# Output projections that take the activations as the stationary operand, with a token-major residual

## The chip, the cores and the metric

The kernel runs on one core of one Trainium2 chip, as one program. The metric is the device time of one execution in microseconds (us). Half speed of TensorE's clock is 1.2 GHz, full speed 2.4 GHz; the profile shows the granted clock as a share of the full one.

## The reference

Two transformer blocks are applied to one sequence of 256 tokens with 2048 features, all in fp32. The first block's shift, scale and gate vectors come from a condition vector `c`. Cut to what matters here:

```
mod = silu(c) @ ada_w + ada_b                 # 6 vectors of 2048: sh_a, sc_a, g_a, sh_f, sc_f, g_f
h = rms_norm(x, pre) * (1 + sc_a) + sh_a
y = mixer(h)                                  # w_in, latent and differential heads, then concat @ w_o
x = x + g_a * rms_norm(y, attn_post)
h = rms_norm(x, ffn_pre) * (1 + sc_f) + sh_f
u = conv3(h @ w_up); y = (gelu(u_gate) * u_val) @ w_down
x = x + g_f * rms_norm(y, ffn_post)
h = rms_norm(x, norm_g)                       # second block
x = x + concat(heads_a, heads_b)(h @ w_in_2) @ w_out
return rms_norm(x, final_g)
```

The matrices that matter are `w_o` (2048x2048), `w_down` (5632x2048) and `w_out` (2048x2048): the output projections. rms_norm needs the sum of squares over the 2048 features of each token.

## The kernel before

All weights come as one stream, `wstream`, in 704 pieces of 512 KB, each eight blocks of 128x128, in the order of use, through SP's DMA queue (`fetch`, L268) into twelve buffers `raw`. `convert` splits each chunk of four blocks into a rounded part `hi` (ACT, L290) and a remainder `lo` (DVE, L291), four chunks ahead of the matmuls; six such pairs of buffers exist. The activations have the same two parts, side by side in one tile of 128 features by 512 (256 tokens rounded, 256 tokens remainder). A product takes three passes: hi by hi, hi by remainder, lo by hi.

Three helpers issue matmuls. `mm3` (L329 to L331) holds the weight block still and streams 256 tokens three times. `mmw` (L337, L338) does the same with one 512-wide and one 256-wide pass. `job_n` (L421 to L423) holds 128 tokens of the activations still and streams 512 columns of weights; only the value projection uses it. `job_t` goes column by column of the output, `job_ko` keeps several columns open and goes over the contraction tiles `kt` outside, so that work can start when only the first `kt` exist.

The residual `x` is kept feature-major, as the products of `mm3` come out: eight tiles of 128 features by two times 256 tokens. An output projection comes in two halves over its contraction: `y_first` copies the first half from PSUM to `accy` (L1131), `y_second` adds the second half (`y_stats`, L1154). `y_stats` then makes three sets of squares and products (ACT L1158 and L1163, DVE L1159), which TensorE sums over features by matmuls with a matrix of ones (L1168), and scales `y` by gate and norm weight (L1171). For each pair of output columns this is one group, and the sums of all groups gather in one PSUM tile `st`. `post` turns them by small selection matmuls (L1180) into per-token numbers, takes two inverse roots (`rsqrt_fast`, L552 to L557) and broadcasts them (L567). `make_h` with `x_new` (L1224 to L1226) then updates `x` and makes the input `h` of the next projection, two feature tiles at a time, at every even `kt` of the `job_ko` that starts w_up and w_in_2 (ACT L1211, L1212 and DVE L1213 in the first, L1206 and L1207 in the second). The last stage, w_out, adds into `x` (L1413, L1426), squares (L1427), sums by ones (L580), scales (L1434), and `fin` multiplies eight tiles and stores them (L1448, L1449).

The gate vectors are made among other work: `ada_late` is woven into w_o, `ada_dve` with `ada_fold` (L526) into w_up.

Work of the engines is recorded in program order: each engine does its instructions strictly in the order in which a generator of the body issued them (`tick` advances such generators as matmuls are issued).

Of the kernel before, what the change touches and what calls it, by code (L numbers as in the profile page):

```python
# [13 lines left out]
F32 = mybir.dt.float32  # L14
# [3 lines left out]
AF = mybir.ActivationFunctionType  # L18
# [3 lines left out]
P = 128  # L22
T = 256
# [8 lines left out]
KO = 4  # L32
LATE, VSLOT = 4, (1,2, 3)
# [101 lines left out]
class Body:  # L135
# [293 lines left out]

    def ada_pe(self, slots, n, done=None, vec=()):  # L430
# [5 lines left out]
        def unit(m, kt):  # L436
            def fn(wt, o):
# [8 lines left out]
                if last and kt == KT - 1 and e == n * 128:  # L446
                    self.spawn(self.ada_end(box["ps"], slots, n, done), "ada")
# [62 lines left out]
    def ada_dve(self, part, t0):  # L510
        out, box = [], {}
        for kt in range(KT):
            def fn(wt, o, kt=kt):
# [3 lines left out]
                if kt == KT - 1 and o * 128 + wt.shape[-1] == 512:  # L517
                    self.spawn(self.ada_fold(box["acc"], part * 16 + t0), "ada")
# [3 lines left out]
    def ada_fold(self, acc, col):  # L522
# [536 lines left out]
    def p_attn(self):  # L1059
# [59 lines left out]
    def y_job(self, mat, kts, x, ko, ev):  # L1119
        cols = [128 * i for i in range(16)]  # L1120
        out = self.job_ko(mat, cols[:ko], kts, x, ev) if ko else []
        return out + self.job_t(mat, cols[ko:], kts, x, lambda i, ps: ev(ko + i, ps))

    def y_first(self, mat, kts, x, ko=0):
        self.accy = None

        def ev(i, ps):
            if i == 0:
                self.accy = [None] * 8
            self.accy[i // 2] = d = self.g()  # L1130
            self.nc.scalar.copy(d, ps)  # L1131
        return self.y_job(mat, kts, x, ko, ev)

    def y_second(self, mat, kts, x, part, wname, ko=0):
        nc = self.nc
        V, S = nc.vector, nc.scalar

        def start():
            self.gw = self.s(16)
            V.tensor_tensor(out=self.gw, in0=self.mod[:, part * 16:part * 16 + 16], in1=self.vec(wname), op=ALU.mult)  # L1140
            self.st = self.ps()
            self.load_sqrt()

        def ev(i, ps):
            self.spawn(self.y_stats(i, ps), "y")
        return self.call(start) + self.y_job(mat, kts, x, ko, ev)

    def y_stats(self, i, ps):
        nc = self.nc
        V, S = nc.vector, nc.scalar  # L1150
        y = self.accy[i // 2]
        hv = [slice(h * T, h * T + T) for h in range(2)]
        for a in (hv if i == 14 else [slice(0, 512)]):
            V.tensor_add(y[:, a], y[:, a], ps[:, a])  # L1154
        yq, zq, xz = self.w(), self.w(), self.w()
        for h, a in enumerate(hv):
            gw = self.gw[:, i + h:i + h + 1]
            S.activation(zq[:, a], y[:, a], AF.Square, scale=gw)  # L1158
            V.scalar_tensor_tensor(out=xz[:, a], in0=y[:, a], scalar=gw, in1=self.x[i // 2][:, a],  # L1159
                                   op0=ALU.mult, op1=ALU.mult)  # L1160
            if i == 14 or h == 1:
                b = a if i == 14 else slice(0, 512)
                S.activation(yq[:, b], y[:, b], AF.Square)  # L1163
        if i != 14:
            yield
        for h, b in enumerate(hv):
            for j, a in enumerate((yq, zq, xz)):
                nc.tensor.matmul(self.st[32 * j:32 * j + 32, :T], self.cst("ones", 0, 32), a[:, b],  # L1168
                                 start=i + h == 0, stop=i + h == 15, tile_position=(0, 32 * j))
        for h, a in enumerate(hv):  # L1170
            S.activation(y[:, a], y[:, a], AF.Identity, scale=self.gw[:, i + h:i + h + 1], bias=0.0)  # L1171

    def post(self):
        nc = self.nc
        V = nc.vector
        part = self.w()
        V.tensor_copy(part[:96, :T], self.st[:96, :T])
        ps = self.ps()
        for t in range(2):
            nc.tensor.matmul(ps[:, t:t + 6:2], part[:96, t * 128:t * 128 + 128], self.cst("sel", 1, 4)[:96],  # L1180
                             start=True, stop=True)
        ry = self.rsqrt_fast(ps[:, 0:2], 2, 1.0 / D)
        t = self.s(2)
        V.tensor_tensor(out=t, in0=ps[:, 2:4], in1=ry, op=ALU.mult)
# [585 lines left out]
```

## Time and profile before

| | |
|---|---|
| median of 3 runs | 1730.6 us (1730.32 to 1730.95) |
| the profiled execution, its span | 1729.1 us, 1727.3 us |
| busy: PE, DVE, ACT | 98%, 70%, 55% of the span |
| mean granted clock of TensorE | 0.988 |
| HBM read, written | 373.06 MB, 2.10 MB |

The span runs from the first to the last recorded event; what lies around it is 1.8 us. PE's busy time counts matmuls as pipelined work; the duration of one matmul in a row is its latency, so rates are read from the distance of the starts. The rows used are in the section ahead of the prediction.

### The profile page before, as it was taken

Reading aid. Unit: us, or ns where it says so; the run is one execution under the profiler, and the core shown is the slowest. Engines: PE = TensorE matmul, PEld = TensorE weight load, DVE = VectorE, ACT = ScalarE, POOL = GpSimd, SP = SyncE. Lnnn points to the kernel's source line nnn. Section 1 sums busy time; section 2 is a strip of 40 time slices with the busy share of each in tenths; the row PEclk is TensorE's granted clock in tenths of the full one; section 3 lists DMA queues with packets and bytes.
Section 4 is the critical chain, followed back from the end, with each engine's and each line's share of the span. In section 5 each row is a group of like instructions: output and inputs, shape, how many; then the busy total and the mean of one; then the engine's idle time right before and its main releaser. Section 6 shows DMA issues by size and latency. Waiting matters only on the chain.

```text
span 1727.3 us, 31993 instructions
## 1 busy us (share of the span) xinstructions
PE 1687.2 (98%) x12008; PEld 1468.4 (85%) x12008; DVE 1215.4 (70%) x2472; ACT 948.5 (55%) x1975; POOL 8.9 (1%) x25
## 2 busy tenths in 40 slices
PE   6999999999989999999999999999989999999997
PEld 4778877788779888899998888899989888888996
DVE  7666678777578978865568777755576767777654
ACT  4444458654567766654456666654544445555553
POOL 0000000000000000000000000000000000000000
PEclk8999999999989999999999999999989999999998
DMA  9978885879945766666676765555445773443431
GB/s 381 338 283 302 305 292 184 286 304 375 345 161 185 235 223 219 221 224 217 204 232 223 226 196 185 194 172 173 168 145 184 255 252 110 142 138 136 141 128 50
DMA packets 104987, 377.24 MB, mean 218 GB/s; under 512 B 11776, under 2 KB 12032, under 8 KB 104832
## 3 DMA queue, kind: packets, MB, share of 16 engines
q1 hardware_dynamic: 103968, 373.51, 62.6%
q8 instruction: 94, 1.54, 0.4%
q10 hardware_dynamic: 864, 1.69, 0.3%
q14 instruction: 61, 0.50, 0.1%
HBM read 373.06 MB, written 2.10 MB: 217 GB/s over the span
## 4 chain that ended last, share of the span: by engine, by line
PE 96%; DVE 2%; DMA 1%; ACT 0%; issue 0%; ACTq 0%; DVEq 0%
PE ps L337 24%; PE ps L329 14%; PE ps L330 14%; PE ps L331 14%; PE ps L338 12%; PE ps L444 4%; PE ps L421 2%; PE ps L422 1%; PE ps L423 1%; PE ps L646 1%; PE ps L1168 1%; PE ps L1639 1%; PE ps L952 1%; PE ps L1660 1%; PE ps L1589 1%; PE ps L769 1%
## 5 line engine op out<-in xcount | busy, mean ns | idle before, releaser
L290 ACT CAST hi<-raw 128x512 fp32r<-128x512 f32 x989 | 608.9, 620 | 585.8 <-PE ps L330 270.4
L291 DVE TENSOR_TENSOR lo<-raw,hi 128x512 fp32r<-128x512 f32 x989 | 673.8, 689 | 315.6 <-ACT hi L290 308.8
L337 PE MATMUL ps<-g,hi 128*128 128x512 f32 x1744 | 619.0, 399 | 0.0
L329 PE MATMUL ps<-g,hi 128*128 128x256 f32 x1968 | 569.2, 290 | 4.0 <-ACT g L1211 2.1
L330 PE MATMUL ps<-g,hi 128*128 128x256 f32 x1968 | 559.3, 284 | 0.0
L331 PE MATMUL ps<-g,lo 128*128 128x256 f32 x1968 | 558.0, 284 | 0.0
L338 PE MATMUL ps<-g,lo 128*128 128x256 f32 x1744 | 489.5, 281 | 0.0
L329 PEld LDWEIGHTS ps<-g,hi 128*128 128x128 f32 x1968 | 378.3, 193 | 44.6 <-issue 18.0
L337 PEld LDWEIGHTS ps<-g,hi 128*128 128x128 f32 x1744 | 327.4, 188 | 80.4 <-issue 1.7
L330 PEld LDWEIGHTS ps<-g,hi 128*128 128x128 f32 x1968 | 379.2, 193 | 5.7 <-issue 4.3
L331 PEld LDWEIGHTS ps<-g,lo 128*128 128x128 f32 x1968 | 378.8, 193 | 2.9 <-issue 2.1
L338 PEld LDWEIGHTS ps<-g,lo 128*128 128x128 f32 x1744 | 329.6, 189 | 0.0
L487 DVE SCALAR_TENSOR_TENSOR w<-raw,csil,w 128x512 f32<-128x512 f32 x105 | 78.6, 749 | 30.9 <-DMA raw<-wstream 30.2
L444 PE MATMUL ps<-raw,cz 128*32 128x512 f32 (+1 forms) x608 | 79.9, 564 | 0.0
L884 DVE TENSOR_TENSOR g<-g,ps 128x512 f32<-128x512 f32 (+1 forms) x48 | 31.8, 664 | 43.7 <-PE ps L331 43.6
L421 PE MATMUL ps<-hi,g 128*128 128x512 f32 (+1 forms) x136 | 51.8, 381 | 1.1 <-ACT g L845 1.1
L422 PE MATMUL ps<-lo,g 128*128 128x512 f32 (+1 forms) x136 | 49.9, 367 | 0.0
L423 PE MATMUL ps<-hi,g 128*128 128x512 f32 (+1 forms) x136 | 49.8, 366 | 0.0
L1239 ACT ACTIVATE w<-w,vt 128x256 f32<-128x256 f32 x80 | 47.7, 599 | 1.9 <-DVE w L345 1.6
L345 DVE TENSOR_TENSOR w<-w,ps 128x256 f32<-128x256 f32 x109 | 45.0, 415 | 0.8 <-ACT w L344 0.8
L649 ACT ACTIVATE w<-ps,t 128x256 f32<-128x256 f32 (+1 forms) x80 | 33.5, 429 | 19.9 <-DVE t L1031 15.6
L344 ACT COPY w<-ps 128x256 f32<-128x256 f32 x109 | 40.1, 369 | 0.0
(266 smaller groups left out, 1257.4 us busy)
## 6 DMA issues: line engine op xcount, KB each, us to landing
raw<-wstream SPq DMA_DIRECT2D x704, 512.0 KB, 4.3
g<-xt SPq DMA_DIRECT2D x8, 256.0 KB, 5.5
out<-g SPq DMA_DIRECT2D x8, 256.0 KB, 2.4
g<-ropes ACTq DMA_DIRECT2D x2, 256.0 KB, 2.5
vt<-vecs ACTq DMA_DIRECT2D x1, 459.5 KB, 4.2
ct<-cst ACTq DMA_DIRECT2D x1, 265.0 KB, 3.1
g<-w ACTq DMA_DIRECT2D x1, 256.0 KB, 3.2
g<-pos SPq DMA_DIRECT2D x1, 160.0 KB, 3.8
```

What stands on the lines that cost most here:

```text
L290: self.nc.scalar.copy(hi[:, :n], src)
L291: self.nc.vector.tensor_sub(lo[:, :n], src, hi[:, :n].bitcast(F32))
L329: i = mm(o, hi, x[:, :T], start=first, stop=False)
L330: mm(o, hi, x[:, T:], start=False, stop=False)
L331: mm(o, lo, x[:, :T], start=False, stop=last)
L337: mm(ps, hi, x, start=first, stop=False)
L338: mm(ps[:, T:], lo, x[:, :T], start=False, stop=last)
L421: mm(ps[t][:, c], xh, hi, start=f and o == 0, stop=False)
L422: mm(ps[t][:, c], xh, lo, start=False, stop=False)
L423: mm(ps[t][:, c], xl, hi, start=False, stop=l and c.stop == w)
L444: mm(box["ps"][32 * q:32 * q + 32, o * 128:e], self.cz[:, a:a + 32], wt, start=first, stop=last and kt >= 12 and e == n * 128, tile_positi ...
L487: V.scalar_tensor_tensor(out=a, in0=w, scalar=c, in1=a, op0=ALU.mult, op1=ALU.add)
```

## The change

The three output projections go to a new helper `job_y`, of the form of `job_n`: 128 tokens of activations are stationary and 512 columns of weights move, six matmuls for four blocks, 1216 blocks in all. Outputs come out token-major, so the residual is kept token-major (`xn`, eight tiles of 128 tokens by 512 features), and is loaded anew in that form by eight DMAs (`load_x`). The statistics become sums along a row: ACT's square and DVE's multiply write them with an accumulator (`accum_out`), and three small reductions replace the matmuls with ones. Gate and norm weight now run along a row, so they are made as broadcast rows `gw` by 512-wide fp32 matmuls (`ada_rows`, `ada_fold`), from rows loaded by DMA. `x_new` works on rows; `x_turn` transposes four 128x128 pieces on TensorE to get back to features for `h`, at odd `kt`, one pair of tiles ahead. The first half of w_down ends after 26 contraction tiles in place of 22.

```diff
...
+YK = 26
...
+    def job_y(self, mat, groups, kts, x, evac):
+        out = []
+        kts = list(kts)
+        box = {}
+        for n, kt in enumerate(kts):
+            for g in groups:
+                def fn(wt, o, n=n, kt=kt, g=g):
+                    mm = self.nc.tensor.matmul
+                    hi, lo = wt
+                    f, l = n == 0, n == len(kts) - 1
+                    if f and o == 0:
+                        box[g] = [self.ps() for _ in range(2)]
+                    c = slice(o * 128, o * 128 + hi.shape[-1])
+                    xk = x(kt)
+                    for t in range(2):
+                        xh, xl = xk[:, t * 128:t * 128 + 128], xk[:, T + t * 128:T + t * 128 + 128]
+                        ps = box[g][t]
+                        mm(ps[:, c], xh, hi, start=f and o == 0, stop=False)
+                        mm(ps[:, c], xh, lo, start=False, stop=False)
+                        mm(ps[:, c], xl, hi, start=False, stop=l and c.stop == 512)
+                    if l and c.stop == 512:
+                        for t in range(2):
+                            self.later(lambda t=t, ps=box[g][t]: evac(g, t, ps))
+                out.append(U("w", 4, mat, kt, 512 * g, fn, True))
+        return out
...
+    def gate_start(self, j):
+        self.gw = [self.g() for _ in range(4)]
+        for n in range(4):
+            self.nc.sync.dma_start(self.gw[n], self.io["rows"][4 * j + n])
+        self.brow = self.g()
+        self.nc.sync.dma_start(self.brow, self.io["brow"][j])
+        self.gdone = [False] * 4
+
+    def ada_rows(self, ps):
+        nc = self.nc
+        self.gate_start(0)
+        sb = self.w()
+        nc.vector.tensor_tensor(out=sb, in0=self.brow, in1=ps, op=ALU.add)
+        yield
+        for n in range(4):
+            ps2 = self.ps()
+            nc.tensor.matmul(ps2, self.cst("jsel", n, n + 1).to_broadcast([P, P]), sb, start=True, stop=True)
+            yield
+            nc.vector.tensor_tensor(out=self.gw[n], in0=self.gw[n], in1=ps2, op=ALU.mult)
+            self.gdone[n] = True
+
+    def ada_fold(self, acc, n):
+        nc = self.nc
+        a = slice(32 * n, 32 * n + 1)
+        if n == 0:
+            self.gate_start(1)
+        nc.vector.tensor_tensor(out=acc[a], in0=acc[a], in1=self.brow[a], op=ALU.add)
+        yield
         ps = self.ps()
-        for j in range(4):
-            nc.tensor.matmul(ps[:, j:j + 1], acc[:, j * 128:j * 128 + 128], self.cst("ones", 0, 1),
-                             start=True, stop=True)
-        yield
-        nc.vector.tensor_add(self.mod[:, col:col + 4], ps[:, :4], self.vec("ada_b", col, col + 4))
+        nc.tensor.matmul(ps, self.cst("ones"), acc, start=True, stop=True)
+        yield
+        nc.vector.tensor_tensor(out=self.gw[n], in0=self.gw[n], in1=ps, op=ALU.mult)
+        self.gdone[n] = True
...
+        def load_x():
+            self.x = None
+            self.xn = {}
+            for n in range(4):
+                for t in range(2):
+                    self.xn[n, t] = d = self.g()
+                    nc.sync.dma_start(d, self.io["xn"][4 * t + n])
+
         oT = lambda k: self.need(lambda: self.oT[k])
         prog += self.call(start_mla)
-        prog += _weave(self.y_first("w_o", range(8, 16), oT, 8), self.ada_late(20, 36), 8)
-        prog += _weave(self.y_second("w_o", range(8), oT, 2, "attn_post", 8), self.ada_late(36, 48), 8)
+        prog += self.align()
+        prog += _weave(self.y_first("w_o", range(8, 16), oT, [[0, 1], [2], [3]]), self.ada_late(20, 36), 8)
+        prog += self.call(load_x)
+        prog += _weave(self.y_second("w_o", range(8), oT, [[0, 1], [2], [3]]), self.ada_late(36, 48), 8)
...
+    def y_second(self, mat, kts, x, groups):
+        def start():
+            self.sy, self.szz, self.sxz = self.s(8), self.s(8), self.s(8)
+            self.load_sqrt()
+
+        def ev(n, t, ps):
+            self.spawn(self.y_stats(n, t, ps), "y")
...
+        y = self.accy[n, t]
+        c = slice(4 * t + n, 4 * t + n + 1)
...
+        V.tensor_add(y, y, ps)
+        while not self.gdone[n]:
...
+        j1, j2, z = self.w(), self.w(), self.g()
+        S.activation(j1, y, AF.Square, accum_out=self.sy[:, c])
+        V.tensor_tensor(out=z, in0=y, in1=self.gw[n], op=ALU.mult)
+        self.accy[n, t] = z
+        S.activation(j1, z, AF.Square, accum_out=self.szz[:, c])
+        V.scalar_tensor_tensor(out=j2, in0=z, scalar=2.0, in1=self.xn[n, t], op0=ALU.mult, op1=ALU.mult,
+                               accum_out=self.sxz[:, c])
+
...
+        sy, sxz, szz = self.rowsum(self.sy), self.rowsum(self.sxz), self.rowsum(self.szz)
+        ry = self.ry = self.rsqrt_fast(sy, 2, 1.0 / D)
         t = self.s(2)
-        V.tensor_tensor(out=t, in0=ps[:, 2:4], in1=ry, op=ALU.mult)
-        V.scalar_tensor_tensor(out=t, in0=ps[:, 4:6], scalar=2.0, in1=t, op0=ALU.mult, op1=ALU.add)
+        V.tensor_tensor(out=t, in0=szz, in1=ry, op=ALU.mult)
+        V.tensor_tensor(out=t, in0=sxz, in1=t, op=ALU.add)
         V.tensor_tensor(out=t, in0=t, in1=ry, op=ALU.mult)
         V.tensor_tensor(out=self.sxx, in0=self.sxx, in1=t, op=ALU.add)
-        r1 = self.rsqrt_fast(self.sxx, 2, 1.0 / D)
+        self.r1 = self.rsqrt_fast(self.sxx, 2, 1.0 / D)
...
+    def x_new(self, i):
+        V = self.nc.vector
+        n, o = i // 2, (i % 2) * T
+        xr = self.xr[i] = self.w()
+        with self.tc.issue_after(self.rs.ins):
+            for t in range(2):
+                x, z = self.xn[n, t], self.accy[n, t]
+                if i < 2 or o == 0:
+                    a = slice(o, o + T) if i < 2 else slice(0, 512)
+                    V.scalar_tensor_tensor(out=x[:, a], in0=z[:, a], scalar=self.ry[:, t:t + 1], in1=x[:, a],
+                                           op0=ALU.mult, op1=ALU.add)
+                V.tensor_scalar(out=xr[:, t * T:t * T + T], in0=x[:, o:o + T], scalar1=self.r1[:, t:t + 1], scalar2=None,
+                                op0=ALU.mult)
+
+    def x_turn(self, i, al, sh):
+        nc = self.nc
+        V, S = nc.vector, nc.scalar
+        xr = self.xr.pop(i)
...
+        for j in range(2):
+            for t in range(2):
+                self.transpose(ps[:, j * T + t * 128:j * T + t * 128 + 128], xr[:, t * T + j * 128:t * T + j * 128 + 128])
         for j in range(2):
             k = 2 * i + j
-            xn = z[:, j * T:j * T + T]
+            src = ps[:, j * T:j * T + T]
...
+                f = xr[:, j * T:j * T + T]
+                S.activation(h[:, :T], src, AF.Identity, bias=b, scale=a)
+                S.activation(f, src, AF.Identity, bias=b, scale=a)
+                V.tensor_sub(h[:, T:], f, h[:, :T].bitcast(F32))
...
+    def make_h(self, kt, al, sh):
+        if kt == 0:
+            self.x_new(0)
+            self.x_turn(0, al, sh)
+        if kt % 2 == 0 and kt < 14:
+            self.x_new(kt // 2 + 1)
+        if kt % 2 == 1 and kt < 15:
+            self.x_turn(kt // 2 + 1, al, sh)
...
+        prog += _weave(up(KO, YK) + self.y_first("w_down", range(YK), gx, each) + up(YK, 44),
                        sum([self.ada_dve(5, 4 * c) for c in range(4)], []), 20)
-        prog += self.call(lambda: self.drain("ada"))
-        prog += self.y_second("w_down", range(22, 44), gx, 5, "ffn_post")
+        prog += self.call(lambda: self.drain("ada")) + self.align()
+        prog += self.y_second("w_down", range(YK, 44), gx, each)
...
+        def ev2(n, t, ps):
+            x = self.xn[n, t]
+            c = slice(4 * t + n, 4 * t + n + 1)
+            V.tensor_add(x, x, ps)
             sq = self.w()
-            for a in ([slice(0, T), slice(T, 512)] if i == 14 else [slice(0, 512)]):
-                V.tensor_add(x[:, a], x[:, a], ps[:, a])
-                S.activation(sq[:, a], x[:, a], AF.Square)
-
-            def f():
-                for h in range(2):
-                    self.sumsq_mm(self.st, sq[:, h * T:h * T + T], i + h, 16)
-                for h in range(2):
-                    a = x[:, h * T:h * T + T]
-                    S.activation(a, a, AF.Identity, scale=self.vec("final_g", i + h, i + h + 1), bias=0.0)
-            self.later(f)
-        prog += wo(range(8, 16), ev2)
+            S.activation(sq, x, AF.Square, accum_out=self.sy[:, c])
+            o = self.xn[n, t] = self.g()
+            V.tensor_tensor(out=o, in0=x, in1=self.fg[n], op=ALU.mult)
...
+            r = self.rsqrt_fast(self.rowsum(self.sy), 2, 1.0 / D)
+            for i, (n, t) in enumerate(sorted(self.xn)):
+                a = self.xn[n, t]
+                if i % 3 == 2:
+                    S.activation(a, a, AF.Identity, scale=r[:, t:t + 1], bias=0.0)
+                else:
+                    V.tensor_scalar(out=a, in0=a, scalar1=r[:, t:t + 1], scalar2=None, op0=ALU.mult)
+                nc.sync.dma_start(self.io["out"][4 * t + n], a)
...
...
```

On PE, in w_down's second half, the stream before has the six matmuls with ones (`ct`) behind a group of columns, here among the products of the next (`ps` is the output, then stationary or moving operands as the program lists them):

```order
L329 MATMUL ps_13666<-g_11773,hi_13610 128x256
L330 MATMUL ps_13666<-g_11773,hi_13610 128x256
L331 MATMUL ps_13666<-g_11773,lo_13611 128x256
L1168 MATMUL ps_13453<-w_13680,ct 32x256
L1168 MATMUL ps_13453<-w_13681,ct 32x256
L1168 MATMUL ps_13453<-w_13682,ct 32x256
L1168 MATMUL ps_13453<-w_13680,ct 32x256
L1168 MATMUL ps_13453<-w_13681,ct 32x256
L1168 MATMUL ps_13453<-w_13682,ct 32x256
L329 MATMUL ps_13666<-g_11892,hi_13628 128x256
L330 MATMUL ps_13666<-g_11892,hi_13628 128x256
L331 MATMUL ps_13666<-g_11892,lo_13629 128x256
```

After the change the place between one group of 512 columns and the next, whose two output tiles are for the two halves of the tokens:

```order
L449 MATMUL ps_12946<-hi_13102,g_12785 128x512
L450 MATMUL ps_12946<-lo_13103,g_12785 128x512
L451 MATMUL ps_12946<-hi_13102,g_12785 128x512
L449 MATMUL ps_12947<-hi_13102,g_12785 128x512
L450 MATMUL ps_12947<-lo_13103,g_12785 128x512
L451 MATMUL ps_12947<-hi_13102,g_12785 128x512
L449 MATMUL ps_13162<-hi_13114,g_10672 128x512
L450 MATMUL ps_13162<-lo_13115,g_10672 128x512
L451 MATMUL ps_13162<-hi_13114,g_10672 128x512
L449 MATMUL ps_13163<-hi_13114,g_10672 128x512
L450 MATMUL ps_13163<-lo_13115,g_10672 128x512
L451 MATMUL ps_13163<-hi_13114,g_10672 128x512
```

The matmuls with ones have gone from the stream, and each operand pair now serves 512 columns.

On DVE, the end of w_o before the change: the last adds and products, the copy of the sums (L1177) and the first small operation:

```order
L1154 TENSOR_TENSOR g_5333<-g_5333,ps_6051 128x256 x2
L1159 SCALAR_TENSOR_TENSOR w_6135<-g_5333,s_5346,g_90 128x256 x2
L291 TENSOR_TENSOR lo_6220<-raw_5897,hi_6219 128x512
L1177 COPY w_6152<-ps_5348 96x256
L552 TENSOR_SCALAR t_6157<-ps_6154 128x2
L554 RECIPROCAL t_6158<-t_6159 128x2
L555 SCALAR_TENSOR_TENSOR t_6159<-t_6158 128x2
```

and after it, where L1208 are the adds, L1213 the products with the gate row, L1216 the multiply-sums, L1221 the reductions and L606 the first small operation:

```order
L1208 TENSOR_TENSOR g_5161<-g_5161,ps_5617 128x512
L1208 TENSOR_TENSOR g_5163<-g_5163,ps_5618 128x512
L1213 TENSOR_TENSOR g_5713<-g_5161,g_4287 128x512
L293 TENSOR_TENSOR lo_5799<-raw_5529,hi_5798 128x512
L1216 SCALAR_TENSOR_TENSOR w_5712,t_5192<-g_5713,g_5186 128x512
L1213 TENSOR_TENSOR g_5721<-g_5163,g_4287 128x512
L1221 TENSOR_REDUCE t_5728<-t_5190 128x2
L1216 SCALAR_TENSOR_TENSOR w_5720,t_5192<-g_5721,g_5188 128x512
L1221 TENSOR_REDUCE t_5730<-t_5192 128x2
L1221 TENSOR_REDUCE t_5732<-t_5191 128x2
L606 TENSOR_SCALAR t_5734<-t_5728 128x2
```

The sums now stand on DVE itself, with a conversion (L293) between them.

On SP, after the change, in w_o, the loads of the token-major `x` stand between pieces of the weight stream:

```order
L270 DMA raw_5168<-wstream 128x1024
L270 DMA raw_5172<-wstream 128x1024
L1159 DMA g_5174<-xn 128x512
L1159 DMA g_5176<-xn 128x512
L1159 DMA g_5178<-xn 128x512
L1159 DMA g_5180<-xn 128x512
L1159 DMA g_5182<-xn 128x512
L1159 DMA g_5184<-xn 128x512
L1159 DMA g_5186<-xn 128x512
L1159 DMA g_5188<-xn 128x512
L270 DMA raw_5211<-wstream 128x1024
L270 DMA raw_5224<-wstream 128x1024
L270 DMA raw_5228<-wstream 128x1024
```

Eight loads that the stream before did not have, 2 MB together, stand ahead of the next piece.

On ACT and then on DVE, after the change, in w_up's k-outer part, the work of one `x_turn` (L1272, L1273 and L1274) stands between conversions (L292, L293):

```order
L292 CAST hi_6001<-raw_5579 128x512
L292 CAST hi_6017<-raw_5579 128x512
L1272 ACTIVATE g_5993<-ps_5988,mod,s_5726 128x256
L1273 ACTIVATE w_5951<-ps_5988,mod,s_5726 128x256
L1272 ACTIVATE g_5997<-ps_5988,mod,s_5726 128x256
L1273 ACTIVATE w_5951<-ps_5988,mod,s_5726 128x256
L292 CAST hi_6040<-raw_5589 128x512
L292 CAST hi_6056<-raw_5589 128x512
```

```order
L293 TENSOR_TENSOR lo_6018<-raw_5579,hi_6017 128x512
L1249 TENSOR_SCALAR w_6035<-g_5182,t_5749 128x256
L1274 TENSOR_TENSOR g_5993<-w_5951,g_5993 128x256
L1249 TENSOR_SCALAR w_6035<-g_5184,t_5749 128x256
L1274 TENSOR_TENSOR g_5997<-w_5951,g_5997 128x256
L293 TENSOR_TENSOR lo_6041<-raw_5589,hi_6040 128x512
L293 TENSOR_TENSOR lo_6057<-raw_5589,hi_6056 128x512
```

The scalings read the transposes out of PSUM (`ps_5988`), and DVE's L1249 prepares the next pair in between.

## Rows read from the trace of the kernel before

**Rows 1.** The page: busy time of each engine, and the chain by engine.
```profile
PE 1687.2 (98%) x12008; PEld 1468.4 (85%) x12008; DVE 1215.4 (70%) x2472; ACT 948.5 (55%) x1975; POOL 8.9 (1%) x25
...
PE 96%; DVE 2%; DMA 1%; ACT 0%; issue 0%; ACTq 0%; DVEq 0%
```
**Rows 2.** Timeline of PE in w_down: start, duration, then the instruction.
```profile
799.87 0.28 PE L329 MATMUL ps<-g,hi 128*128 128x256 f32 x1
...
801.31 0.28 PE L329 MATMUL ps<-g,hi 128*128 128x256 f32 x1
```
**Rows 3.** Timeline of PE in the value projection.
```profile
332.08 0.39 PE L422 MATMUL ps<-lo,g 128*128 128x512 f32 x1
...
334.39 0.39 PE L423 MATMUL ps<-hi,g 128*128 128x512 f32 x1
```
**Rows 4.** Timeline of PE in w_up.
```profile
655.84 0.40 PE L337 MATMUL ps<-g,hi 128*128 128x512 f32 x1
...
657.60 0.40 PE L337 MATMUL ps<-g,hi 128*128 128x512 f32 x1
```
**Rows 5.** Timeline of DVE, w_down's second half: the first and last of eight adds.
```profile
1141.13 0.69 DVE L1154 TENSOR_TENSOR g<-g,ps 128x512 f32<-128x512 f32 x1 [0.21 <-PE ps L331]
...
1260.22 0.75 DVE L1154 TENSOR_TENSOR g<-g,ps 128x256 f32<-128x256 f32 x2 [0.21 <-PE ps L331]
```
**Rows 6.** Timeline of DVE, w_out: adds without (L1413) and with statistics (L1426).
```profile
1662.04 0.69 DVE L1413 TENSOR_TENSOR g<-g,ps 128x512 f32<-128x512 f32 x1 [0.22 <-PE ps L331]
1667.80 0.69 DVE L1426 TENSOR_TENSOR g<-g,ps 128x512 f32<-128x512 f32 x1 [0.21 <-PE ps L331]
...
1706.80 0.69 DVE L1426 TENSOR_TENSOR g<-g,ps 128x512 f32<-128x512 f32 x1 [1.66 <-PE ps L331]
```
**Rows 7.** Timeline of PE in the heads: transposes, then fp32 matmuls.
```profile
306.18 0.60 PE L646 MATMUL ps<-ct,w 128*128 128x128 f32 x4
306.62 1.88 PE L952 MATMUL ps<-g,g 128*128 128x512 f32 x4
```
**Rows 8.** Timeline of PE in w_up: one fold of a gate vector.
```profile
657.96 0.95 PE L526 MATMUL ps<-ct,w 128*128 128x1 f32 x8
```
**Rows 9.** Timeline of the gap after w_o.
```profile
485.44 0.28 PE L331 MATMUL ps<-g,lo 128*128 128x256 f32 x1
...
486.42 0.87 DVE L1159 SCALAR_TENSOR_TENSOR w<-g,s,g 128x256 f32<-128x256 f32 x2
...
489.62 0.16 DVE L552 TENSOR_SCALAR t<-ps 128x2 f32<-128x2 f32 x1 [0.70 <-PE ps L1180]
...
492.65 0.16 DVE L557 SCALAR_TENSOR_TENSOR t<-t,t 128x2 f32<-128x2 f32 x1
...
496.14 1.22 PE L329 MATMUL ps<-g,hi 128*128 128x256 f32 x4 [2.06 <-ACT g L1211]
```
**Rows 10.** Groups by line: count, then busy time and mean ns of one.
```profile
L649 ACT ACTIVATION_READ_ACCUMULATOR w<-ps,t 128x1 f32 x80 | 16.1, 201 | 0.0
```
**Rows 11.** Timeline of the gap after w_down.
```profile
1263.01 1.28 ACT L553 ACT_TABLE_LOAD   x1
```
**Rows 12.** Windows in w_o and after it: engines' busy time, granted clock, DMA share, GB/s.
```profile
383.00:456.00 73.00, 73.00 (x560) 58.71 (x559) 50.16 (x84) 35.76 (x71) 0.00 (x0) 1.00 0.97 373
491.40:501.70 10.30, 7.04 (x32) 6.36 (x31) 7.36 (x19) 3.82 (x9) 0.00 (x0) 0.50 0.01 2
```
**Rows 13.** Timeline of the tail.
```profile
1712.98 0.28 PE L331 MATMUL ps<-g,lo 128*128 128x256 f32 x1
...
1716.33 0.16 DVE L552 TENSOR_SCALAR t<-ps 128x2 f32<-128x2 f32 x1 [0.70 <-PE ps L1444]
...
1717.36 0.16 DVE L557 SCALAR_TENSOR_TENSOR t<-t,t 128x2 f32<-128x2 f32 x1
...
1718.90 4.87 DVE L1448 TENSOR_TENSOR g<-g,ps 128x512 f32<-128x512 f32 x8 [1.38 <-PE ps L567]
```
**Rows 14.** Waits of ACT from 300 to 500 us: total, times, longest.
```profile
ACT hi L290 <- DMA raw<-wstream: 13.3, 10, 2.1
```

More of the change, by code (lines that the diff above doesn't have):

```diff
@@ L446, in fn @@
                 if last and kt == KT - 1 and e == n * 128:
-                    self.spawn(self.ada_end(box["ps"], slots, n, done), "ada")
+                    end = self.ada_rows(box["ps"]) if slots[0][0] == 2 else self.ada_end(box["ps"], slots, n, done)
+                    self.spawn(end, "ada")
             return fn
@@ L1134, in y_second, with y_job, y_first, ev @@
-    def y_second(self, mat, kts, x, part, wname, ko=0):
+    def y_job(self, mat, kts, x, groups, ev):
+        return sum([self.job_y(mat, g, kts, x, ev) for g in groups], [])
+    def y_first(self, mat, kts, x, groups):
+        def ev(n, t, ps):
+            if not self.accy:
+                self.accy = {}
+            self.accy[n, t] = d = self.g()
+            self.nc.scalar.copy(d, ps)
+        return self.y_job(mat, kts, x, groups, ev)
+    def y_second(self, mat, kts, x, groups):
+        def start():
+            self.sy, self.szz, self.sxz = self.s(8), self.s(8), self.s(8)
+            self.load_sqrt()
+        def ev(n, t, ps):
+            self.spawn(self.y_stats(n, t, ps), "y")
+        return self.call(start) + self.y_job(mat, kts, x, groups, ev)
@@ L1135, in y_second, with y_stats @@
+    def y_stats(self, n, t, ps):
         nc = self.nc
         V, S = nc.vector, nc.scalar
[L1138 to L1148, printed above, removed]
+        y = self.accy[n, t]
[10 more added lines that the diff above has]
+                               accum_out=self.sxz[:, c])
@@ L1164, in y_stats @@
-        if i != 14:
-            yield
[L1166 to L1177, printed above, removed]
-        ps = self.ps()
[L1179 to L1183, printed above, removed]
-        V.tensor_tensor(out=t, in0=ps[:, 2:4], in1=ry, op=ALU.mult)
-        V.scalar_tensor_tensor(out=t, in0=ps[:, 4:6], scalar=2.0, in1=t, op0=ALU.mult, op1=ALU.add)
-        V.tensor_tensor(out=t, in0=t, in1=ry, op=ALU.mult)
-        V.tensor_tensor(out=self.sxx, in0=self.sxx, in1=t, op=ALU.add)
-        r1 = self.rsqrt_fast(self.sxx, 2, 1.0 / D)
-        ps = self.ps()
-        self.ryb = self.bcast_mm(ry, ps, 0)
-        self.r1b = self.bcast_mm(r1, ps, 1)
-        self.hs = {}
@@ L1408, in p_block2, with ev1 @@
             prog += self.call(go)
[L1410 to L1415 removed]
+        yT = lambda k: self.need(lambda: self.yT[k])
+        def ev1(n, t, ps):
+            x = self.xn[n, t]
+            V.tensor_add(x, x, ps)
@@ L1417, in mid2 @@
         def mid2():
-            self.st = self.ps()
+            self.fg = [self.g() for _ in range(4)]
+            for n in range(4):
+                nc.sync.dma_start(self.fg[n], self.io["rows"][8 + n])
+            self.sy = self.s(8)
             self.load_sqrt()
-        prog += self.call(mid2)
-        def ev2(i, ps):
-            x = self.x[i // 2]
+        def ev2(n, t, ps):
+            x = self.xn[n, t]
+            c = slice(4 * t + n, 4 * t + n + 1)
+            V.tensor_add(x, x, ps)
```

109 lines of the change are left out of this document (34 added, 75 removed).

## The prediction

> **What bounds the kernel now.** I read the page first, then the chain, then single stages. TensorE is busy for 98% of the span, and the chain of work that ended last lies on it for 96% [rows 1]. So the time is the sum of what PE issues, plus the three places where PE has nothing to issue: after w_o, after w_down, and the tail. Everything the change does is therefore priced by PE issue spacing where PE runs, and by the serial chain of small operations where it doesn't. The durations printed for matmuls are latencies and overlap; what counts is the distance between starts.
>
> In w_down the old form starts a 128x256 matmul every 0.120 us: twelve steps from 799.87 to 801.31 [rows 2]. Three passes make 0.360 us a block of weights. The value stage of the attention already has the form that the change uses everywhere, activations stationary and 512 columns of weights moving: ten steps from 332.08 to 334.39 take 2.31 us, 0.231 each [rows 3]. Six of these do four blocks: 6 x 0.231 / 4 = 0.3465 us a block.
>
> The profiled run took 1729.1 us, its span 1727.3, and the median of the three runs is 1730.6, which is 1.5 above the profiled one. I sum against 1729.1 and add 1.5 at the end. A change of under 0.2% (3.5 us) can't be told from none here.
>
> **The change, term by term.**
>
> A, matmul form. w_o (256 blocks), w_down (704) and w_out (256) go to the new form: 1216 x (0.360 - 0.3465) = -16.4 us. The bound from the nearest other row: a pair of one 512 and one 256 matmul in w_up takes 1.76 us for five pairs, 0.352 [rows 4]; less 0.120 for the 256 leaves 0.232, which is 0.348 a block and -14.6. Conversions don't stop it: a chunk of four blocks now lasts 1.39 us on PE in place of 1.44, and takes one DVE and one ACT operation of 128x512, where an add of that size took 0.69 [rows 5].
>
> B, statistics on PE. Before, each pair of output tiles in the second halves is followed by six matmuls with ones (12 records). w_down's second half has adds from 1141.13 to 1260.22, seven steps, 17.01 each [rows 5], against 44 x 0.360 = 15.84 for the matmuls alone: 1.17 a pair. Seven pairs in w_down and seven in w_o (the eighth lies in the gap): 14 x 1.17 = -16.4. In w_out the step grows from 5.76 (1662.04 to 1667.80) to 6.50 (six steps, 1667.80 to 1706.80) [rows 6]: 7 x 0.74 = -5.2. Now these sums are made by ACT's and DVE's accumulators and PE sees nothing of it. The cover is that these engines run beside PE with room: per group of two tiles (25 us in w_down's second half, 18 x 4 x 0.3465) they get 2 adds, 2 products, 2 multiply-sums and 4 squares, about 4 us on DVE and 3.5 on ACT. If the cover went, a late conversion would cost PE at most one such burst a group.
>
> C, transposes back. Fourteen groups of four 128x128 transposes stand in the matmul stream of w_up and w_in_2 (two more lie in the gaps). A group of four takes from 306.18 to 306.62, 0.44 [rows 7]: 14 x 0.44 = +6.2. Their consumers (two to four ACT scalings out of PSUM, two DVE subtractions) must be ready when the next pair of k tiles begins; I count no wait for that and price it as a rival.
>
> D, gate rows. Eight fp32 matmuls of 128x512 make the broadcast gate rows. Four records, two matmuls, took 1.88 [rows 7]: 8 x 0.94 = 7.5. Out go the four folds (0.95 each, 8 records [rows 8]) and one fold of the same eight records, 4.75. Net +2.8 (2 to 4).
>
> E, the two gaps. After w_o, PE's last matmul starts at 485.44 and the next useful one at 496.14: 10.7 us, through add, squares, ones-matmuls, copy, selection matmul, the small operations (489.62 to 492.65 and 0.16 behind it, 3.19), broadcast, three DVE operations, ACT [rows 9]. The new path counted from the same point: two 512 adds, a product, a late lo-conversion, the first multiply-sum, second product and multiply-sum at 0.6 to 0.75 each, ends at 4.5; the accumulator read (0.2 [rows 10]) and a reduction, 4.8; the same small operations, 8.0; four x_new operations at 0.435 (two take 0.87 [rows 9]), 9.7; four transposes, 10.3; ACT, 11.0. So the second adds, products and sums replace six PE round trips and come out nearly even: +0.4. After w_down the same, and the 1.28 us load of ACT's table, which now falls beside squares and PSUM matmuls [rows 11], may enter the chain: +1.1. Sum +1.5, bounds -2 to +6. In the gap the granted clock fell to 0.50 from 491.4 to 501.7 [rows 12], the lower of the two levels (1.2 GHz); the 5.6 us of matmuls in it ran at half speed, worth 2.8. I assume that both kernels pay this.
>
> F, the tail. From the last matmul at 1712.98: broadcast done and first scaling at 1718.90, 5.9 us, with eight scalings over 4.87 us behind it [rows 13]. Without the ones-matmuls, copy, selection and broadcast, the add, square, reduction and the root's 1.2 (1716.33 to the operation that starts at 1717.36 [rows 13]) end at about 3.8; eight scalings, six on DVE and two on ACT, gain some more, but 2 MB must leave behind them, and 2 MB at the 373 GB/s of a full stretch [rows 12] is 5.6 us. That floor makes the gain -2.5 (0 to -4.6).
>
> G, more data in a full stretch. The token-major x is loaded by eight DMAs of 256 KB on SP's queue between two weight pieces, in w_o. DMA is at 0.97 of its share there [rows 12] and ACT's casts already waited 13.3 us for pieces in that part [rows 14], though PE did not. The 2 MB delay the stream by 5.6 us; PE's lead over conversions covers most of it, and the burst of four evacuations of the first double group lies in the same place. +3 (0 to 8).
>
> Sum: -16.4 - 16.4 - 5.2 + 6.2 + 2.8 + 1.5 - 2.5 + 3.0 = -27.0. 1729.1 - 27.0 = 1702.1; in medians 1703.6, which I call 1703.
>
> A rule to weigh against this is in the Trainium skill, "TensorE: Matmul & The Clock Gate", section "Back-to-back issue gap": its table has 262 cycles at 2.4 GHz for 256 columns and 518 for 512, so 109.2 and 215.8 ns. By that the new form saves 3 x 109.2 - 1.5 x 215.8 = 3.9 ns a block, 4.7 us in all in place of 16.4. The trace disagrees with both figures, 0.120 and 0.231 us.
>
> **The rivals.**
>
> 1. Late pieces in w_o cost more than 3. For it: the full DMA share and the casts that waited. Against: PE had no wait there, and the stream catches up within the stage. At 8 to 14 us in place of 3 the time is 1709 to 1715.
>
> 2. The form saves less. Spacing may be split into a part per column and a part per start: 0.231 - 0.120 = 0.111 for 256 columns leaves 0.009 a start, and a block has 3 starts before and 1.5 now, which is the 0.0135. If the true part per start is a quarter to a third of that (the 0.231 is from one stretch of another stage, with other loads ahead of its matmuls), A is -4 to -5.5 in place of -16.4 and the time about 1715. Rows 2 and 3 speak against it, and nothing in the trace for it. The Trainium skill's rule above gives this result too.
>
> 3. Slower than before: h depends on PE. In w_up's k-outer part a k tile lasts 8 x 0.36 = 2.88 us. Its transposes stand one k tile ahead of use, and behind them in strict order ACT does up to four scalings of 0.6 and DVE two subtractions among conversions, some 2.0 to 2.6 us. If ACT is held by a cast that waits for a buffer, PE waits, then conversions are late too, and the loss repeats at all 14 groups. It takes 27 / 14 = 1.9 us a group to eat the gain, and 2.2 to be slower than before by 0.2%: about 1734 and up. Against: by my count 0.3 to 0.9 us are left, and w_in_2's k tiles are longer (12 blocks, 4.3 us).
>
> 4. The gaps shrink more than I count and the clock falls later: E and F together at their low bounds, -3.5 and -2.1 below the sum, G at nothing: 3.5 + 2.1 + 3.0 less, 1695.
>
> **How the numbers follow.** The sum with G from 0 to 6 and its neighbours 0.60; rival 1 0.13; rival 2 0.08; rival 3 0.08, of which a fraction ends within 0.2%; rival 4 0.11. The range 1692 to 1716 takes in rivals 1, 2 and 4 (with D, too, at its best 1694, and 2 us for the scatter of what w_o's statistics cost among its other work) and leaves out rival 3. Within the likeliest case alone it is 1697 to 1709. Faster by over 0.2%: 0.88; same 0.04; slower 0.08.
>
> **What would show it.** After: starts 0.231 apart in w_down (rows of the new matmul lines); steps between evacuations in w_down of 26 x 4 x 0.3465 = 36.0 and 18 x 4 x 0.3465 = 24.9 with nothing of PE's between; gaps of 10.5 to 12.5 us; 0.44 for a group of transposes and no PE wait ahead of the next k tile; DMA waits of casts in w_o that reach PE by under 6 us; a tail of 11 to 13 us. The prediction is wrong if the new spacing is 0.24, if PE waits for ACT's h in each pair of k tiles, or if PE idles for pieces in w_o for more than 8 us.

## The result, and the profile after

The changed kernel takes 1709.2 us in the median of four runs (1705.07 to 1710.42) against 1730.46 before: a ratio of 0.9875, interval 0.9856 to 0.9893, which is 21.3 us less. 1703 was predicted, with a range of 1692 to 1716. The sign and the size are right within the range; the 6 us between are more than the interval allows (it begins at 1705.5), and the largest error behind them is a wait that the sum didn't have at all.

The page of the profiled run (1710.42 us, span 1708.5), to be held against [rows 1]:

```profile
PE 1652.9 (97%) x9968; PEld 1363.4 (80%) x9968; DVE 1222.6 (72%) x2499; ACT 929.8 (54%) x1949; POOL 9.1 (1%) x25
...
PE 93%; DVE 3%; DMA 2%; ACT 1%; issue 0%; ACTq 0%; SPq 0%; DVEq 0%
```

PE is still the chain, but three points of it have gone to others. The new form on PE in w_down, ten steps from one row to the other (timeline), beside [rows 2, 3]:

```profile
1194.91 0.39 PE L451 MATMUL ps<-hi,g 128*128 128x512 f32 x1
...
1197.17 0.39 PE L449 MATMUL ps<-hi,g 128*128 128x512 f32 x1
```

That is 0.226 a start, not the 0.231 of the value projection: 0.339 us a block. The adds of w_down's second half show it at a longer range (timeline of DVE), beside [rows 5]:

```profile
1201.36 1.28 DVE L1208 TENSOR_TENSOR g<-g,ps 128x512 f32<-128x512 f32 x2
1225.84 1.28 DVE L1208 TENSOR_TENSOR g<-g,ps 128x512 f32<-128x512 f32 x2
1250.32 1.28 DVE L1208 TENSOR_TENSOR g<-g,ps 128x512 f32<-128x512 f32 x2
```

24.48 us a step is 18 x 4 x 0.340, with nothing of PE's beside the matmuls. The first gap, a group of transposes with the matmul behind it, and the tail's first part, to be held against [rows 7, 9, 13] (timeline):

```profile
492.73 0.39 PE L451 MATMUL ps<-hi,g 128*128 128x512 f32 x1
...
501.99 1.16 PE L700 MATMUL ps<-ct,w 128*128 128x128 f32 x4 [8.87 <-DVE w L1249]
...
503.81 0.58 PE L331 MATMUL ps<-g,hi 128*128 128x256 f32 x1 [0.66 <-ACT g L1272]
...
515.00 0.60 PE L700 MATMUL ps<-ct,w 128*128 128x128 f32 x4
515.36 0.36 PE L331 MATMUL ps<-g,hi 128*128 128x256 f32 x1
...
1696.51 0.39 PE L451 MATMUL ps<-hi,g 128*128 128x512 f32 x1
1700.16 2.47 DVE L1499 TENSOR_SCALAR g<-g,t 128x512 f32<-128x512 f32 x6
```

Transposes cost 0.36 a group, the first gap 11.1 us, the tail 12.0. Those went nearly as forecast. The part that did not lies in w_o, at 333 us, where PE had no wait before (timeline):

```profile
328.13 2.10 SPq L554 DMA_DIRECT2D g<-rows  x4
...
331.20 0.33 SPq L556 DMA_DIRECT2D g<-brow  x1
...
332.50 0.39 PE L425 MATMUL ps<-hi,g 128*128 128x512 f32 x1
...
338.39 0.69 DVE L563 TENSOR_TENSOR w<-g,ps 128x512 f32<-128x512 f32 x1 [2.68 <-DMA g<-brow]
...
339.23 1.19 PE L567 MATMUL ps<-w,ct 128*128 128x512 f32 x1 [6.34 <-DVE t L594]
```

`ada_rows` issues its five loads and, next in DVE's order, the add that needs the last of them. The load lands 7 us later, behind the weight pieces that were under way. The first broadcast matmul (L567) stands next in PE's order and waits for that add: 6.3 us with PE empty. The windows show what follows (engines' busy time, granted clock, DMA share, GB/s; the first row is for the start of the program, told below):

```profile
28.00:34.00 6.00, 4.35 (x17) 3.32 (x14) 4.50 (x12) 3.13 (x6) 0.00 (x0) 0.72 1.02 406
333.00:336.00 3.00, 0.00 (x0) 0.00 (x0) 1.29 (x2) 2.23 (x8) 0.00 (x0) 1.00 1.03 397
336.00:339.20 3.20, 0.00 (x0) 0.00 (x1) 0.77 (x3) 0.39 (x1) 0.00 (x0) 0.77 0.74 257
339.20:342.00 2.80, 2.77 (x4) 1.17 (x4) 2.45 (x14) 0.00 (x0) 0.00 (x0) 0.50 0.03 13
342.00:345.00 3.00, 3.00 (x11) 0.50 (x10) 1.33 (x3) 0.00 (x0) 0.00 (x0) 0.58 0.00 0
```

With PE empty the granted clock falls to 0.50, the lower level, and stays there for some 5 us of PE's work (all of 339.2 to 342, most of 342 to 345). The stream stops, since no piece is used up: 0.03 of the DMA engines' time and less, where it was 1.03 just before. SP's longest wait from 328 to 350 us (total, times, longest) is for the matmuls that read raw weights and stand behind the broadcasts on PE:

```profile
SPq L270 <- PE ps L472: 8.8, 1, 8.8
```

By stages, from the first row of each (start until the first matmul of `mm3`, input projection until the first head, from there to w_o's last matmul, gap, w_up and w_down, gap, second block to its last matmul, tail):

| | start | input | heads, w_o | gap | w_up, w_down | gap | block 2 | tail |
|---|---|---|---|---|---|---|---|---|
| before | 35.7 | 212.3 | 237.5 | 10.7 | 763.8 | 10.6 | 442.4 | 14.3 |
| after | 38.9 | 212.3 | 241.6 | 11.1 | 746.2 | 12.0 | 434.5 | 12.0 |

By the sum's terms for it (A -3.5, B -8.2, D +2.8, G +3.0) the stretch with w_o should have become 6 us shorter; it became 4 longer. The start, which has the same instructions in both, lost 3 us too.

### The profile page after: what moved, and what is told of

Read it like the earlier page. It is cut to its first block, busy times and chain, and to the rows that moved or that the text cites. A ratio compares the mean times of both kernels' runs of the same rounds, so it can differ in the third digit from the quotient of the medians.

```text
span 1708.5 us, 27826 instructions
## 1 busy us (share of the span) xinstructions
PE 1652.9 (97%) x9968; PEld 1363.4 (80%) x9968; DVE 1222.6 (72%) x2499; ACT 929.8 (54%) x1949; POOL 9.1 (1%) x25
## 4 chain that ended last, share of the span: by engine, by line
PE 93%; DVE 3%; DMA 2%; ACT 1%; issue 0%; ACTq 0%; SPq 0%; DVEq 0%
PE ps L339 24%; PE ps L340 12%; PE ps L449 8%; PE ps L450 8%; PE ps L451 8%; PE ps L331 6%; PE ps L332 5%; PE ps L333 5%; PE ps L472 4%; PE ps L700 2%; PE ps L423 2%; PE ps L424 1%; PE ps L425 1%; DVE lo L293 1%; PE ps L1690 1%; PE ps L1006 1%
## 5 line engine op out<-in xcount | busy, mean ns | idle before, releaser
L292 ACT CAST hi<-raw 128x512 fp32r<-128x512 f32 x989 | 610.0, 622 | 588.9 <-PE ps L339 194.0
L293 DVE TENSOR_TENSOR lo<-raw,hi 128x512 fp32r<-128x512 f32 x989 | 672.7, 689 | 308.9 <-ACT hi L292 303.7
L340 PE MATMUL ps<-g,lo 128*128 128x256 f32 x1744 | 489.8, 281 | 0.0
L339 PEld LDWEIGHTS ps<-g,hi 128*128 128x128 f32 x1744 | 327.6, 188 | 82.8 <-issue 2.4
L340 PEld LDWEIGHTS ps<-g,lo 128*128 128x128 f32 x1744 | 329.6, 189 | 0.8 <-issue 0.7
L449 PE MATMUL ps<-hi,g 128*128 128x512 f32 x608 | 240.9, 398 | 1.5 <-ACT hi L292 1.5
L450 PE MATMUL ps<-lo,g 128*128 128x512 f32 x608 | 237.1, 390 | 0.6 <-DVE lo L293 0.6
L451 PE MATMUL ps<-hi,g 128*128 128x512 f32 x608 | 237.1, 390 | 0.0
L331 PE MATMUL ps<-g,hi 128*128 128x256 f32 x752 | 220.9, 296 | 1.2 <-ACT g L1272 0.7
L332 PE MATMUL ps<-g,hi 128*128 128x256 f32 x752 | 214.0, 285 | 0.0
L333 PE MATMUL ps<-g,lo 128*128 128x256 f32 x752 | 213.7, 285 | 0.0
L331 PEld LDWEIGHTS ps<-g,hi 128*128 128x128 f32 x752 | 144.9, 194 | 24.5 <-ACT hi L292 12.4
L332 PEld LDWEIGHTS ps<-g,hi 128*128 128x128 f32 x752 | 145.5, 194 | 2.4 <-issue 1.4
L333 PEld LDWEIGHTS ps<-g,lo 128*128 128x128 f32 x752 | 145.3, 193 | 0.8 <-issue 0.8
L449 PEld LDWEIGHTS ps<-hi,g 128*128 128x128 f32 x608 | 113.7, 188 | 39.5 <-issue 7.8
L450 PEld LDWEIGHTS ps<-lo,g 128*128 128x128 f32 x608 | 114.2, 188 | 25.9 <-DVE lo L293 2.7
L451 PEld LDWEIGHTS ps<-hi,g 128*128 128x128 f32 x608 | 114.1, 188 | 24.1
L700 PE MATMUL ps<-ct,w 128*128 128x128 f32 x248 | 37.8, 279 | 18.8 <-DVE w L1249 18.8
```

The source lines that it names most:

```text
L292: self.nc.scalar.copy(hi[:, :n], src)
L293: self.nc.vector.tensor_sub(lo[:, :n], src, hi[:, :n].bitcast(F32))
L331: i = mm(o, hi, x[:, :T], start=first, stop=False)
L332: mm(o, hi, x[:, T:], start=False, stop=False)
L333: mm(o, lo, x[:, :T], start=False, stop=last)
L339: mm(ps, hi, x, start=first, stop=False)
```

## The experiments

Each kernel ran beside the kernel before on the same chip. Differences between my kernels are taken from their ratios to it, times 1730; differences of stages are taken between profiles, one execution each.

**The changed kernel again**, unedited.

> The changed kernel unedited, beside the others on one chip. My theory: the 3.2 us that it lost in the first 34 us is TensorE's clock, which stayed at the lower level for 10 us longer there though the instructions are the same, so that this profile may come back without it; the stall at the first gate row (6.3 us of PE idle) must come back in every run. Expected 1705 to 1711 us. Rival: the loss at the start belongs to the change and is there again.

Ratio 0.9877 (0.9862 to 0.9892), 1708.42 us. The start took 36.7 in place of 38.9, PE's idle at the gate row 6.9, the stretch to w_o's end 242.2. So the stall is the kernel's. At the start the first profile of after has a granted clock of 0.72 from 28 to 34 us (window above). The best kernel of this study, the last one told below, has it too in its profile:

```profile
28.00:34.00 6.00, 4.38 (x14) 3.56 (x15) 4.71 (x12) 3.12 (x6) 0.00 (x0) 0.72 1.02 406
```

The late add, which does the same work there, has 1.00. So the loss at the start is not the change's: over thirteen profiles the start lasts 35.7 to 38.9 us, in no order that follows the edits.

**The add later.**

```diff
         self.gate_start(0)
+        for _ in range(10):
+            yield
         sb = self.w()
```

> The add of the gate bias row on DVE is recorded ten ticks (about 40 blocks) later, the loads stay where they are. Theory (DVE stood behind one add that waited for a load, and casts, remainders and PE behind it): PE's idle 6.3 us at 333 to 339 goes and the time falls by 4 to 7 us. Rival (w_o is bound by the weight stream, so that whatever is saved there is waited for later): the stall goes but w_o ends within 2 us of where it did, time within 2 us of the changed kernel.

1698.27 us, ratio 0.9818 (0.9803 to 0.9832): 10.2 us less than the changed kernel beside it, well over the 4 to 7 of my theory. A second time:

> The late add once more, unedited, beside the next two on one chip: 1695 to 1700 us, 9 to 12 us faster than the changed kernel, with no idle of PE at the first gate row.

1699.62, ratio 0.9822, 9.5 us less than the changed kernel. The same windows as above, in the first profile of the late add:

```profile
28.00:34.00 6.00, 4.96 (x30) 3.72 (x34) 5.83 (x13) 3.93 (x7) 0.00 (x0) 1.00 1.02 405
333.00:336.00 3.00, 3.00 (x28) 1.06 (x27) 2.61 (x15) 1.45 (x3) 0.00 (x0) 1.00 1.04 401
336.00:339.20 3.20, 3.20 (x22) 2.31 (x15) 1.24 (x3) 1.20 (x3) 0.00 (x0) 1.00 1.03 410
339.20:342.00 2.80, 2.80 (x15) 2.17 (x13) 2.80 (x6) 0.78 (x2) 0.00 (x0) 1.00 1.03 407
```

The loads are where they were; PE is busy, the clock full and the stream full. The stretch to w_o's end is 232.1 us in place of 242.2, so the wait cost 10.1: 6.9 of idle, and some 3 us by which the matmuls behind it, most of them at the half clock, took longer. In the second profile of the late add the stretch is 232.3. The rival, that w_o's stream would eat the gain, falls.

**The awaited load first.**

```diff
         self.gw = [self.g() for _ in range(4)]
+        self.brow = self.g()
+        self.nc.sync.dma_start(self.brow, self.io["brow"][j])
         for n in range(4):
             self.nc.sync.dma_start(self.gw[n], self.io["rows"][4 * j + n])
-        self.brow = self.g()
-        self.nc.sync.dma_start(self.brow, self.io["brow"][j])
```

> The changed kernel with one edit: the load of the gate bias row, which DVE's add waits for, is issued ahead of the four norm-weight rows in place of behind them; the add stands where it stood. Theory (the wait is for that load's turn in the queue): the load is issued some 3 us earlier, so PE's idle falls from 6.3 to 3 or 4 us and the time by 3 to 5 us, about half of what the late add gives. Rival (the wait is for the stretch's transfers as a whole): same within 1 us of the changed kernel.

1702.82, ratio 0.9838 (0.9825 to 0.9852), 6.7 us less than the changed kernel run again. PE's waits from 320 to 350 us (total, times, longest) have 4.3 us, against 6.9 there:

```profile
PE ps L567 <- DVE t L594: 4.3, 1, 4.3
```

The theory's mechanism is right: the idle falls by about what it said. The gain is over its 3 to 5, but only 3.7 of it lies in heads and w_o (238.5 us against 242.2); another 3.4 lies in w_up and w_down, where PE's wait for the second gate's row (1.0 us in the changed kernel run again) is gone and the rest is no more than profiles of one kernel differ by (743.8 and 746.4 for the late add). Heads and w_o are 6.4 over the late add for 4.3 of idle, where it was 10.1 for 6.9: a wait here costs about one and a half times its idle.

**x loaded early.**

```diff
             prog += self.align() + self.call(lambda g=g: self.drain("ada", f"h{g}"))
+            if g == last:
+                prog += self.call(self.load_x)
...
-        prog += self.call(load_x)
```

> The eight loads of the token-major x are issued when the last group of the input projection begins, some 100 pieces earlier, in place of the saturated stretch of w_o. Theory (2 MB in a full stretch delay the pieces, PE waits some 2 to 3 us at 459 to 482): 2 to 5 us faster. Rival (the waits there come from the burst of evacuations on DVE): same within 1 us.

1707.82, ratio 0.9871: 1.0 us less, within the intervals. Heads and w_o fell from 242.2 to 240.9 us, the input projection rose from 212.3 to 214.1. The theory falls; the rival's same within 1 us is what came.

> Both edits, the late add and the early load of x. If each cause stands alone: sum of the two, 6 to 11 us faster than the changed kernel, 1698 to 1703. If the stream bounds w_o: less than the larger of the two plus 2.

1701.8, ratio 0.984: 6.4 us faster than the changed kernel, which either reading on record allows, but 3.8 us slower than the late add alone. Heads and w_o take 232.1 as without the early load, and PE's waits there for converted weights are the same: so the 2 MB are free in w_o. The input projection takes 214.0 again: they cost 1.7 us where I put them, in a stretch whose DMA share they raised from 0.75 to 0.98 (200 to 230 us). Another 2.0 of the 3.8 lies in w_up and w_down, within what two profiles of the late add differ by.

**Half the width.** On top of the late add:

```diff
-                        mm(ps[:, c], xh, hi, start=f and o == 0, stop=False)
...
+                        for a in range(0, hi.shape[-1], 256):
+                            b = slice(a, a + 256)
...
+                            mm(ps[:, d], xh, hi[:, b], start=f and o == 0 and a == 0, stop=False)
...
```

> On top of the late add: each 512-wide matmul of the output projections is split into two of 256, same stationary activations, same products, so 12 starts for four blocks in place of 6. Theory (the gain of the new form is in the width of the moving operand: 0.360 us a block at 256 against 0.340 at 512): 1216 x 0.020 = 24 us slower than the late add alone, 1720 to 1725. Rival (the gain is in which operand is stationary, or in two matmuls in a row with the same one): at most 5 us slower.

1717.18, ratio 0.9923 (0.991 to 0.9935): 18 us slower, under the 24 of the theory and far over the rival's 5. In w_down, twelve steps:

```profile
820.05 0.28 PE L452 MATMUL ps<-hi,g 128*128 128x256 f32 x1
...
821.49 0.28 PE L452 MATMUL ps<-hi,g 128*128 128x256 f32 x1
```

0.120 a start, the old form's spacing to the digit, with the new form's stationary operand. The gain is in the width; the rival falls. By stages w_up with w_down are 13.0 longer than in the first late add (10.4 against the second) and block 2 4.8 (5.7), near 14.4 and 5.2; w_o only 2.7 of 5.2.

**Two turns.** On top of the late add, each group of transposes twice (`for j in (0, 1, 0, 1)`).

> On top of the late add: every group of four transposes is done twice into the same tile. Theory (a group costs PE its own 0.36 to 0.44 us and nothing waits behind it): 14 groups and 2 in the gaps, 6 to 7 us slower than the late add alone, 1704 to 1706. Rival (the chain from the transposes to h has no room, so that the next k tile waits): over 10 us slower.

1708.06, ratio 0.9873: 9.5 us slower, between the theory's 6 to 7 and the rival's 10. A group takes 0.79 in place of 0.36:

```profile
505.09 1.04 PE L702 MATMUL ps<-ct,w 128*128 128x128 f32 x8
505.88 0.36 PE L331 MATMUL ps<-g,hi 128*128 128x256 f32 x1
```

14 x 0.43 is 6.0, the two gaps are longer by 0.86 and 0.85, together 7.7; no wait of PE stands ahead of a k tile. The rest of the 9.5 has no place in the profile but a 1.3 us wait at the second gate's row, which other runs have at 0.2 to 1.2, and 1.2 at the start. So 7.7 of it is shown, and the 1.8 above is not.

**The matmuls with ones back.** On top of the late add:

```diff
+        yield
+        for h in range(2):
+            b = slice(h * T, h * T + T)
+            for j, a in enumerate((j1, z, j2)):
+                nc.tensor.matmul(self.st[32 * j:32 * j + 32, :T], self.cst("ones", 0, 32), a[:, b],
...
```

> On top of the late add: behind each tile's statistics in w_o and w_down the six matmuls with ones stand in the stream again, into a PSUM tile that nothing reads (the sums that are used still come from the accumulators). Theory (their whole cost falls on PE): 14 x 1.0 to 1.17 = 14 to 17 us slower than the late add alone. Rival (PE has room among waits in w_o, where the weight stream is full): only w_down's 7 count, 7 to 9 us.

1714.6, ratio 0.9906: 15.2 us slower, as the theory has it. The places are twelve and not fourteen: the profile has 72 records of these matmuls in each of the two streams, six groups of two tiles, and the last two tiles' lie in the gaps, which stay at 11.1 and 12.0 us. Heads and w_o grow by 5.5 us, w_up and w_down by 10.4 against the first late add and 7.8 against the second. So a place cost 1.1 to 1.3 us.

**Smaller bursts, and the second gate.**

```diff
-        prog += _weave(self.y_second("w_o", range(8), oT, [[0, 1], [2], [3]]), self.ada_late(36, 48), 8)
+        prog += _weave(self.y_second("w_o", range(8), oT, [[0], [1], [2], [3]]), self.ada_late(36, 48), 8)
...
             self.gate_start(1)
+            for _ in range(10):
+                yield
```

> On top of the late add: w_o's second half goes group by group, so that two tiles are evacuated at a time in place of four, and the same late add is made for the rows of the second gate in w_up. Theory (PE's 1.2 us wait at the first evacuation of w_o comes from casts behind the statistics of four tiles; the second gate's add holds DVE up by about 1 us): 1 to 3 us faster than the late add alone, 1695 to 1697. Rival (the weight stream is late in any case there): same within 1 us.

1701.07, ratio 0.9832: 2.4 us slower in the medians, not faster; heads and w_o are 4.3 longer. The first evacuation now comes 13 us earlier. There the casts stand on ACT behind statistics that wait for DVE, and DVE does sums with raw weights between (timeline of PE):

```profile
439.55 0.74 PE L449 MATMUL ps<-hi,g 128*128 128x512 f32 x2 [2.85 <-ACT hi L292]
```

> The late add for the second gate too, with w_o's groups as in the changed kernel. Theory (the run with three edits lost in w_o, at the earlier evacuation, and its late add in w_up was worth up to 1 us): 0 to 1.5 us faster than the late add alone. Rival (the later add in w_up runs into other work): slower by over 1 us.

1698.99, ratio 0.981 (0.9796 to 0.9823): the lowest ratio, not to be told from the late add. Its DVE has no wait for `brow` in w_up any more, where the late add alone still had one in both profiles; the second:

```profile
DVE w L579 <- DMA g<-brow: 0.9, 1, 0.9
```

This version beats both kernels: 1.9% under before, 0.7% under the change.

## Why the prediction was right or wrong

The forecast was right on the whole and 6 us off by errors that partly cancelled.

A, matmul form: mechanism right, size too small. -16.4 was from 0.231, read from ten steps in another stage; in w_down's long stretch it is 0.226, so 1216 x 0.0205 = -25 if it held everywhere. In w_o it doesn't (below). The half-width run shows that it is the width. Rival 2, and with it the Trainium skill's rule in "TensorE: Matmul & The Clock Gate", section "Back-to-back issue gap", asked for 1715: it falls. The page gives that table for a matmul by itself; its 215.8 ns for 512 is 10 ns under the spacing measured here and its 109.2 for 256 is 11 under. By the trace alone 256 more columns take 0.226 - 0.120 = 0.106 us, which leaves about 0.014 a start, and 1.5 starts fewer a block make up the gain: the split that rival 2 considered, with a part per start larger than its 0.009 and not smaller.

B, statistics: -16.4 in w_o and w_down, 15.2 measured by putting twelve of the fourteen back. In w_out no run tests it alone, but the second block's stage fits: A -5.2, B -5.2 and seven groups of transposes +2.5 make -7.9, and it went from 442.4 to 434.5.

C, transposes: 0.36 in place of 0.44, 5.0 in all. Rival 3, the sign-changing one, did not come: PE's only wait for `h` in w_up's first part is the 0.7 us at its very start, in w_in_2's the 0.6 at its start, and doubling the groups brought none.

E and F, gaps and tail: +0.4, +1.4 and -2.3 against +0.4, +1.1 and -2.5. So rival 4 didn't come either.

D and G are the step that failed. I priced the gate rows by their eight matmuls, and the new loads by their bytes in w_o's full stretch, with x as the one that counts. I passed over `ada_rows`' own five loads, and named no instruction that waits for one of them and nothing queued behind it. The bytes were nearly free, and the matmuls cheaper than priced (in the late add's profile PE's starts give the folds 3.6 us against 1.8 in w_o, 1.9 against 3.2 in w_up: +0.5 in place of +2.8; my 0.94 a matmul was a printed duration, with the latency in it, where I had meant to go by starts). The wait on one load of 256 KB cost 10 us. +3 for G should have been 0 for x, +10 for `brow` and some 2 for the burst of evacuations (below). Rival 1, late pieces in w_o, had the right stage and the wrong mechanism for this wait: it is not the stream that was late for PE, but PE's and DVE's order that stopped the stream.

Even without the wait w_o falls short. In the late add's profile heads and w_o are 5.4 us shorter than before, where A at 0.226, B and the measured D ask for -5.2 - 8.2 + 1.8 = -11.6. The new form's starts lie 0.250 apart there (383 in 95.6 us; the old form's 767 took 98.1), so that A gave 2.6. Of the missing 6 us 2 are waits of PE for converted weights, which the kernel before doesn't have. They come 2 to 4 us behind the evacuations that start at 445.2 and 465.6 us, with the casts behind the statistics on ACT: the burst that G named (waits of PE, 350 to 480 us, late add):

```profile
PE ps L449 <- ACT hi L292: 1.5, 2, 1.1
PE ps L450 <- DVE lo L293: 0.6, 1, 0.6
```

The start gave up to 3 us more in the first profile, by a clock that no edit moved. So the near hit is in part luck: A at -25, B as priced, C to F as measured, the 10 of the wait and the 6 of w_o make -25.4. The start and w_up's pairs of matmuls (last section), some 3 us each in the profiled run, bring it near the 18.8 us by which that run's span is shorter than before.

What stays open: 1.8 of the 9.5 us of the run with two turns, and what the other 4 us are that w_o falls short by.

## What to carry to other kernels

Where a change adds a load, look for the first instruction that reads it and what stands behind that on its engine: in strict order one add on a fresh 256 KB load held up DVE, PE and the weight stream, and cost three times what eight such loads were priced at. Recording the reader later cost nothing and was worth 10 us, where the change itself had brought 21. A rate should be read from a long stretch of the form alone: a difference of 5 ns a start was a third of the gain. And it holds for such stretches alone: in w_o, among other work, the form gave half of what it gave elsewhere.

## What the runs showed that I had not expected

The granted clock at the start of the program came back to 1.00 anywhere from about 24 to 34 us with the same instructions, which moves the time by up to 3 us. DVE's read of an accumulator takes 0.08 us and ACT's 0.19. The pairs of one 512 and one 256 matmul in w_up ran at 0.353 us in most places and at 0.347 in some stretches of 100 us (680 to 800 in the late add's profile, 1000 to 1130 before the change), at the full clock both times; it moved the stage by 2 to 3 us and I did not find what sets it.
